# One change to the second block of a two-block network on one core: recurrence products as 64x64 pairs, filling products in runs of 12, attention heads in pairs, and the hand-over to the expert stage rearranged

## The chip, the core and the metric

The program runs on one core of a Trainium2 chip. A core has a matrix engine (PE, TensorE), three engines for elementwise work (DVE, ACT, POOL) and SP, which here only issues DMAs. Each engine works through its own list of instructions strictly in the order in which the compiled program holds them; semaphores make one wait for another. The metric is device time in microseconds (us) of one execution of the whole program, the median of the runs shown.

## The reference

Two transformer-like blocks run over 256 tokens of width 1024, in float32. The first (half an FFN, a mixer of long convolution and differential attention, half an FFN) is not touched. The second block, reduced to what matters:

```python
u = rms_norm(x) @ w_in                      # 1920 recurrence columns, q, k, v, 2048 gates
# recurrence, 8 heads of 64, forward and reverse; S is 64x64 per head:
s_kk = S @ kk_t
S = S * w_t - outer(s_kk, a_t * kk_t) + outer(v_t, k_t);  y_t = S @ r_t
y_rwkv = (group_norm(y) * ln_w + ln_b + bonus) * g
# banded attention, 8 query heads of 64, 2 key heads, band of 128, ALiBi, a sink logit
y_attn = softmax_with_sink(q @ k.T + alibi) @ v
merged = sigmoid(g1) * (y_rwkv @ w_proj_rwkv) + sigmoid(g2) * (y_attn @ w_proj_attn)
x = x + merged @ w_out
x = x + expert_choice_moe(rms_norm(x))      # 16 experts, 32 tokens each, 3 weights of 1024x1024
return rms_norm(x)
```

## The kernel before

All activations stand feature by token: a tile is 128 features by 256 tokens. Large products are made exact by splitting: `split` (L138) takes a float32 tile, ACT casts a high part (`whi`, L139), DVE subtracts it (`wlo`, L140), and `mm3` (L142) issues three products (L145 high by high, L146 high by low, L147 low by high). A weight tile of 128 columns and 1024 rows so makes 24 products of 128x128 by 256 columns. `weights` (L125) loads it by one DMA on SP's queue (L130); its raw buffer is free for the next load but one as soon as DVE has made the low part.

**The recurrence** runs in chunks of 64 tokens. For each pair of heads (4 pairs, two heads on partitions 0 to 63 and 64 to 127) and each direction there is a "lane" (`lane`, L1255): decays by a matmul (L1270) and exponentials, products of keys with keys and queries (L1297), transposes (L1308), a triangular inverse (`inverse`, L1363: by blocks of 8 on DVE, then three doubling levels of matmuls), a chain over the four chunks (L1325 to L1345), and the output products. `mm_heads` (L1358) does a product for the two heads as two 64x64 products, one on each half of rows and columns of the array. Where a full 128x128 product is used instead (L1297, L1308, L1387, L1449), the two heads' data stand as diagonal blocks in zero-padded tiles (`bb`, `kh`, filled by ACT at L1291), or all 128 rows are turned at once and the halves copied out one by one (L1310, L1406). `rwkv_out` (L1416) follows each pair's second lane.

**Order.** Four slots hold a lane each; `lanes` (L1197) goes round them, takes one step of each, and after each step spends a credit (`FILL_RATE`) on the "fill": the 22 weight tiles of `w2_fill` (queries, keys and values, gates), 22 x 24 = 528 products that do not depend on the recurrence. `FILL` says in how many pieces a tile's 24 products are handed out. After eight lanes the slots take four attention jobs (`banded`, L1472), each a pair of query heads j and 4+j, one after the other. A list scheduler then sets the final order within each engine; it may pull ready products in between, so pieces of the fill are broken up further.

**Hand-over.** When the lanes end, their SBUF goes to a ring of 27 raw buffers (`moe_raw`), and SP's queue runs on: four tiles `w_proj_rwkv` (into the two old raw buffers), four `w_proj_attn`, eight `w_out`, then the experts' 201 MB in loads of 512 KB. Before the first projection the outputs `ur` and `q` are split (L1054, L1055) into the tiles `h2h` and `h2l`, four small constants are loaded by ACT's queue (L1061, L1064), the router weights `wr` are scaled on DVE (L1065), and the gates go through a sigmoid on ACT in four parts (L1071).

## Time and profile before

| | us |
|---|---|
| median of 3 runs | 1842.15 (1841.99 to 1846.56) |
| the profiled execution | 1840.64 |
| its span, first to last instruction | 1838.9 |
| lane stage, from the 36th fill product to the last | 1086.5 to 1303.3 |
| first `w_proj_attn` load, last `w_proj_rwkv` load | 1303.14, 1309.53 |
| first expert load, last expert load landed | 1317.07, about 1822 |

The profiled execution is one run, 1.5 us below the median; the span leaves out 1.7 us around it. A time such as 1303.15 is us from the span's start. A group of matrix instructions in the timeline merges neighbours of one line and tile; its us reach to the modelled end of the last, so consecutive groups overlap, and what a group cost is read from its start to the next group's start. A float32 product (lines 1270 to 1505) shows as two PE instructions, a transpose and a split product as one. "PEclk" is the granted clock of TensorE, 1.00 for 2.4 GHz, 0.5 for 1.2 GHz.

### The profile page before, as it was taken

What the parts mean: (1) busy time and instruction counts of PE and PEld (TensorE: products, weight loads), DVE (VectorE), ACT (ScalarE), POOL (GpSimd) and SP (SyncE); (2) the same over time, 40 slices, a digit from 0 to 9 for tenths busy, and PEclk for the clock granted to TensorE, in tenths of its full rate; (3) what the DMA queues carried; (4) which work ended last, traced back from release to release, by engine and by line L of the source; (5) the groups of instructions that cost most, each with busy time, mean ns of one, the idle gap of its engine ahead of it and who ended that gap; (6) DMA issues with size and microseconds to landing.
All of it is one profiled execution on the core that took longest, in us unless ns stands there. A gap on an engine that the chain in (4) does not pass through costs nothing.

```text
span 1838.9 us, 33002 instructions
## 1 busy us (share of the span) xinstructions
PE 1704.7 (93%) x13367; PEld 1279.1 (70%) x13367; DVE 1032.4 (56%) x2506; ACT 733.8 (40%) x1576; POOL 19.0 (1%) x37
## 2 busy tenths in 40 slices
PE   8999999999999999999999999999999878787666
PEld 5788787778988889999998888887975222222112
DVE  4888766769977877776657686867751000000001
ACT  4432223647545577475445654555550000000001
POOL 0000000000000000000000000000010000000000
PEclk9999999999999999999999999999999676657887
DMA  8666663324422224545552321111799999999997
GB/s 335 237 212 215 231 243 120 110 92 133 155 95 90 70 89 164 184 183 209 185 176 73 125 98 59 47 44 42 281 400 392 409 408 409 408 409 408 409 408 295
DMA packets 98915, 397.77 MB, mean 216 GB/s; under 512 B 12251, under 2 KB 14924, under 8 KB 85196
## 3 DMA queue, kind: packets, MB, share of 16 engines
q1 hardware_dynamic: 91728, 386.97, 55.9%
q10 hardware_dynamic: 5020, 5.04, 0.9%
q0 software_dynamic: 2016, 3.67, 0.7%
q8 instruction: 105, 1.72, 0.4%
q14 instruction: 46, 0.38, 0.1%
HBM read 394.59 MB, written 1.05 MB: 215 GB/s over the span
## 4 chain that ended last, share of the span: by engine, by line
PE 68%; DMA 21%; DVE 6%; ACT 3%; issue 1%; ACTq 0%; SPq 0%; DVEq 0%
PE mm L145 14%; PE mm L147 13%; PE mm L146 13%; DMA raw<-exp_w_down 7%; DMA raw<-exp_w_gate 6%; DMA raw<-exp_w_up 4%; PE at L145 4%; PE a L1361 4%; PE at L146 4%; PE at L147 4%; PE mm L1530 3%; DMA araw<-w_adat 2%; PE a L1698 2%; DVE ajunk L309 2%; DVE wlo L140 1%
## 5 line engine op out<-in xcount | busy, mean ns | idle before, releaser
L139 ACT CAST whi<-raw 128x512 fp32r<-128x512 f32 x542 | 309.6, 619 | 260.2 <-PE mm L146 126.8
L140 DVE TENSOR_TENSOR wlo<-raw,whi 128x512 fp32r<-128x512 f32 x542 | 356.7, 687 | 89.2 <-ACT whi L139 85.8
L145 PE MATMUL mm<-hh,whi 128*128 128x256 f32 (+1 forms) x784 | 247.8, 317 | 0.4 <-DVE kl L140 0.4
L147 PE MATMUL mm<-hh,wlo 128*128 128x256 f32 (+1 forms) x784 | 247.1, 317 | 0.5 <-DVE wlo L140 0.2
L146 PE MATMUL mm<-hl,whi 128*128 128x256 f32 (+1 forms) x784 | 246.7, 315 | 0.0
L145 PEld LDWEIGHTS mm<-hh,whi 128*128 128x128 f32 x784 | 147.9, 189 | 14.0 <-issue 3.2
L146 PEld LDWEIGHTS mm<-hl,whi 128*128 128x128 f32 x784 | 147.9, 189 | 10.9 <-issue 1.2
L147 PEld LDWEIGHTS mm<-hh,wlo 128*128 128x128 f32 x784 | 147.3, 189 | 10.9 <-DVE wlo L140 1.3
L1665 DVE TENSOR_SCALAR scat<-iota,col 128x256 f32<-128x256 f32 x16 | 6.5, 413 | 260.2 <-PE a L1698 260.2
L1530 PE MATMUL mm<-raw,ehid 128*32 128x256 f32 x960 | 100.7, 515 | 40.6 <-DMA raw<-exp_w_down 40.2
L1702 ACT COPY ys<-mm 128x256 f32<-128x256 f32 (+1 forms) x20 | 7.2, 361 | 318.6 <-PE mm L1530 307.0
L309 DVE SCALAR_TENSOR_TENSOR ajunk<-araw,scr 128x512 bf16<-128x512 f32 x160 | 110.4, 690 | 25.5 <-DMA araw<-w_adat 23.4
L145 PE MATMUL at<-hh,whi 128*128 128x512 f32 (+1 forms) x352 | 119.8, 340 | 0.0
L147 PE MATMUL at<-hh,wlo 128*128 128x512 f32 (+1 forms) x352 | 119.5, 339 | 0.0
L146 PE MATMUL at<-hl,whi 128*128 128x512 f32 (+1 forms) x352 | 119.4, 339 | 0.0
L1530 PE MATMUL mm<-raw,xg 128*32 128x256 f32 x1024 | 101.3, 486 | 12.9 <-DMA raw<-exp_w_gate 12.5
L1530 PE MATMUL a<-raw,xg 128*32 128x256 f32 x1024 | 84.4, 462 | 23.7 <-DMA raw<-exp_w_up 23.7
L145 PE MATMUL mm<-whi,hidh 128*128 128x512 f32 x264 | 105.5, 400 | 0.4 <-DVE y L431 0.3
L147 PE MATMUL mm<-whi,hidl 128*128 128x512 f32 x264 | 105.0, 399 | 0.3 <-DVE hidl L140 0.3
L146 PE MATMUL mm<-wlo,hidh 128*128 128x512 f32 x264 | 105.0, 398 | 0.0
L145 PE MATMUL mm<-h2h,whi 128*128 128x256 f32 x328 | 102.2, 312 | 2.8 <-ACT h2h L988 1.7
L1530 PEld LDWEIGHTS mm<-raw,ehid 128*32 128x32 f32 x960 | 23.5, 123 | 114.5 <-DMA raw<-exp_w_down 96.9
(603 smaller groups left out, 3421.5 us busy)
## 6 DMA issues: line engine op xcount, KB each, us to landing
raw<-exp_w_gate SPq DMA_DIRECT2D x128, 512.0 KB, 10.2
raw<-exp_w_up SPq DMA_DIRECT2D x128, 512.0 KB, 10.2
raw<-exp_w_down SPq DMA_DIRECT2D x120, 512.0 KB, 10.2
raw<-w_ff_in SPq DMA_DIRECT2D x42, 1024.0 KB, 4.8
raw<-w_in SPq DMA_DIRECT2D x32, 1024.0 KB, 4.8
araw<-w_adat SPq DMA_DIRECT2D x56, 512.0 KB, 4.6
raw<-w_ff_out SPq DMA_DIRECT2D x20, 1024.0 KB, 4.8
raw<-w_fill SPq DMA_DIRECT2D x22, 512.0 KB, 3.5
```

The costliest lines, as they stand in the source:

```text
L139: self.high = self.nc.scalar.copy(out=hi, in_=src)
L140: self.low = (eng or self.nc.vector).tensor_tensor(out=lo, in0=src, in1=hi.bitcast(F32), op=ALU.subtract)
L145: nc.tensor.matmul(out=ps, lhsT=w[0], rhs=x[0], start=first, stop=False)
L146: nc.tensor.matmul(out=ps, lhsT=w[0], rhs=x[1], start=False, stop=False)
L147: nc.tensor.matmul(out=ps, lhsT=w[1], rhs=x[0], start=False, stop=last)
L309: nc.vector.scalar_tensor_tensor(out=junk, in0=raw[:, s], scalar=1.0, in1=self.scr[v][:, s], op0=ALU.mult, op1=ALU.mult, accum_out=part[:, ...
L1361: self.nc.tensor.matmul(out=ps[r], lhsT=w[r], rhs=x[r], start=start, stop=stop)
L1530: nc.tensor.matmul(out=ps[q], lhsT=x(k), rhs=raw[:, j, :], start=(k == 0), stop=(k == KT - 1))
L1665: nc.vector.tensor_scalar(out=sc, in0=self.iota[:, 0:T], scalar1=col[:, 0, e:e + 1], scalar2=col[:, 1, e:e + 1], op0=ALU.is_equal, op1=ALU ...
L1698: nc.tensor.matmul(out=acc(tt, j), lhsT=sc[q, tt * 128:tt * 128 + 128], rhs=ys[q], start=False, stop=False)
L1702: nc.scalar.copy(out=ys, in_=ps)
```

## The change

1. **64x64 pairs.** The zero-padded tiles `bb` and `kh` and their eight memsets go; key products use `mm_heads` on `t0` and `t1` directly. Transposes become products with the identity, head by head (`turn_heads`, new). The coefficient product (L1387) and the bonus sum (L1449) become pairs. One copy of 128 partitions stands where there were two of 64.
2. **Last doubling level.** Only half of each 64x64 inverse is still unknown there, so its two products take 32 columns. A tile `ip`, identity plus that half, replaces `P`; POOL writes the identity half, one copy per lane.
3. **Fill.** `FILL, FILL_RATE` go from 4, 0.31 to 2, 0.16: pieces of 12 products instead of 6, half as often. With `whole`, the 2nd to 4th quarter of a piece have high priority in the scheduler, so that it keeps the 12 together.
4. **Attention.** The two heads of a job run together, with products on the two row halves (queries by keys) and the two column halves (by values) side by side in the list, and one copy of the output.
5. **Hand-over.** `h2h`/`h2l` become 16 tiles of 128x256, the outputs are split one such tile at a time, the constants go to POOL's queue, each sigmoid is written where its gates are first used, and `wr` is scaled after the first projection.

```diff
-FILL, FILL_RATE = 4, 0.31
+FILL, FILL_RATE = 2, 0.16
...
-                    self.mm3(ps, (hi[:, k, s], lo[:, k, s]), (x[0][:, k, :], x[1][:, k, :]), k == 0, k == kt - 1)
+                    with self.tc.high_priority() if whole and k % (kt // steps) else ExitStack():
+                        self.mm3(ps, (hi[:, k, s], lo[:, k, s]), (x[0][:, k, :], x[1][:, k, :]), k == 0, k == kt - 1)
...
-            self.split(ur[:, 8:12, :], yr[0], yr[1])
-            self.split(q, ya[0], ya[1])
+            for y, x, i in ((yr, ur, 8), (ya, q, 0)):
+                for k in range(4):
+                    self.split(x[:, i + k, :], y[0][:, k, :], y[1][:, k, :])
...
-            nc.scalar.dma_start(out=t, in_=A[nm])
+            nc.gpsimd.dma_start(out=t, in_=A[nm])
...
-        for dst, src in ((bb, t0), (kh, t1)):
-            for r in HEADS:
-                nc.scalar.copy(out=dst[r, :, r], in_=c4(src)[r])
...
-                nc.tensor.matmul(out=ps[:, c], lhsT=src[:, c, :], rhs=kr[:, :, c * 64:c * 64 + 64], start=True, stop=True)
+                self.mm_heads(ps[:, c], src[:, c, :], kr[:, :, c * 64:c * 64 + 64])
...
-                nc.tensor.transpose(out=ps[:, c, :], in_=src[:, first + c, :], identity=self.ident)
-            for r in HEADS:
-                nc.scalar.copy(out=dst[r, cs], in_=ps[r, :, r])
+                self.turn_heads(ps[:, c, :], src[:, first + c, :])
+            nc.scalar.copy(out=dst[:, cs], in_=ps)
...
+    def turn_heads(self, ps, x):
+
+        for r in HEADS:
+            self.nc.tensor.matmul(out=ps[r], lhsT=x[r], rhs=self.ident[r, r], start=True, stop=True)
...
+        nc.vector.tensor_tensor(out=IP[:, :, src], in0=products(ab, N, src), in1=mask(8)[:, :, src], op=ALU.mult)
+        yield
+        nc.scalar.copy(out=NT[:, :, dst], in_=products(IP, NT, dst))
...
+        for qt in range(2):
+            for g, r in enumerate(HEADS):
+                nc.tensor.matmul(out=ps[g][:, qt, :], lhsT=q[r, j, qt * 128:qt * 128 + 128], rhs=kv[r, 0, :], start=True, stop=True)
```

PE, first lanes, before: 128x128 products and transposes with the padded tiles (`a` is PSUM, `krs` keys and queries, `vtm` the values).

```order
L1297 MATMUL a_10986<-krs_10897,bb_10886 128x128 x4
L1297 MATMUL a_10994<-krs_10897,kh_10888 128x128 x4
L1297 MATMUL a_11077<-krs_10916,bb_10905 128x128 x2
L1308 MATMUL a_11016<-ident,bb_10886 128x128 x3
L1297 MATMUL a_11077<-krs_10916,bb_10905 128x128 x2
L1297 MATMUL a_11099<-krs_10916,kh_10907 128x128
L1308 MATMUL a_11022<-ident,kh_10888 128x128 x3
L1361 MATMUL a_11039<-vtm,ak_10891 64x64 x2
L1297 MATMUL a_11099<-krs_10916,kh_10907 128x128 x3
L1361 MATMUL a_11039<-vtm,kt_10895 64x64 x2
```

The same place now (L1364 is `mm_heads`, L1369 `turn_heads`).

```order
L1364 MATMUL a_10992<-krs_10908,t0s_10910 64x128 x8
L1364 MATMUL a_11004<-krs_10908,t1s_10911 64x128 x8
L1364 MATMUL a_11093<-krs_10926,t0s_10928 64x128 x3
L1369 MATMUL a_11015<-ident,t0s_10910 64x64 x6
L1364 MATMUL a_11093<-krs_10926,t0s_10928 64x128 x4
L1369 MATMUL a_11023<-ident,t1s_10911 64x64 x6
L1364 MATMUL a_11042<-vtm,ak_10901 64x64 x2
L1364 MATMUL a_11093<-krs_10926,t0s_10928 64x128
L1364 MATMUL a_11113<-krs_10926,t1s_10929 64x128 x3
L1364 MATMUL a_11042<-vtm,kt_10905 64x64 x2
```

Every product of this stretch has become 64x64; over the lane stage the neighbours on PE differ in block shape (128x128, 64x64, 64x128, 128x64) 124 times instead of 237, and the 528 fill products stand in 49 runs instead of 101, most of them of 12.

DVE, end of the lanes, before: the low parts of the weights, then `wr`, then the split of `ur` and `q`, then the first projection's output (L1075).

```order
L1454 TENSOR_TENSOR ur<-t0s_10956,a_13781 128x256
L140 TENSOR_TENSOR wlo<-raw,whi 128x512 x4
L1065 TENSOR_TENSOR wr<-wr,pv 128x128
L140 TENSOR_TENSOR h2h<-ur,h2h 128x1024
L140 TENSOR_TENSOR h2l<-q_10151,h2l 128x1024
L140 TENSOR_TENSOR wlo<-raw,whi 128x512
L1075 TENSOR_TENSOR gates<-mm,gates 128x256
L140 TENSOR_TENSOR wlo<-raw,whi 128x512
```

Now (the four `wlo` are the halves of the first two projection tiles, L1470 is the last head pair's output).

```order
L140 TENSOR_TENSOR yl_14041<-q_10165,yl_14037 128x256
L140 TENSOR_TENSOR yl_14042<-q_10165,yl_14038 128x256
L1466 TENSOR_TENSOR t1s_10965<-ur,a_13872 128x256
L140 TENSOR_TENSOR yl_14043<-q_10165,yl_14039 128x256
L1467 TENSOR_TENSOR t0s_10964<-t0s_10964,t1s_10965 128x256
L140 TENSOR_TENSOR yl_14044<-q_10165,yl_14040 128x256
L1470 TENSOR_TENSOR ur<-t0s_10964,a_13877 128x256
L140 TENSOR_TENSOR wlo<-raw,whi 128x512 x4
L140 TENSOR_TENSOR yh_14036<-ur,yh_14032 128x256
L1081 TENSOR_TENSOR gates<-mm,gates 128x256 x2
L1092 TENSOR_TENSOR wr<-wr,pv 128x128
```

Most of the split now stands before the projection's weights, but the last recurrence output has moved behind the end of the fill; 58 fill products are left after the last lane's output products, where 114 were.

SP, the same place, before.

```order
L130 DMA raw<-w_fill 128x1024 x22
L130 DMA raw<-w_proj_rwkv 128x1024 x3
L130 DMA raw<-w_proj_attn 128x1024 x2
L130 DMA raw<-w_proj_rwkv 128x1024
L130 DMA raw<-w_proj_attn 128x1024 x2
L130 DMA raw<-w_out 128x1024 x8
```

Now.

```order
L130 DMA raw<-w_fill 128x1024 x22
L130 DMA raw<-w_proj_rwkv 128x1024 x4
L130 DMA raw<-w_proj_attn 128x1024 x4
L130 DMA raw<-w_out 128x1024 x8
L1545 DMA raw<-exp_w_gate 128x1024 x8
```

Two `w_proj_attn` loads have moved behind the last `w_proj_rwkv` load.

## Rows read from the trace of the kernel before

**Rows 1.** The page: shares of the chain that ended last.

```profile
PE 68%; DMA 21%; DVE 6%; ACT 3%; issue 1%; ACTq 0%; SPq 0%; DVEq 0%
```

**Rows 2.** Windows: us, then busy us (instructions) per engine; clock, DMA share, GB/s.

```profile
1086.50:1303.30 216.80, 212.28 (x2832) 175.90 (x2830) 154.43 (x545) 122.39 (x301) 0.00 (x0) 1.00 0.17 54
1303.30:1309.50 6.20, 4.29 (x22) 3.97 (x21) 4.19 (x6) 2.86 (x5) 0.00 (x0) 0.72 0.72 254
...
1365.00:1400.00 35.00, 34.00 (x353) 21.30 (x355) 12.41 (x39) 8.68 (x18) 5.06 (x8) 0.97 0.98 376
1400.00:1600.00 200.00, 164.80 (x1554) 54.55 (x1550) 9.23 (x22) 5.67 (x15) 0.00 (x0) 0.71 1.03 409
```

**Rows 3.** Timeline of SP's queue: start us, us, line, tile and source.

```profile
1303.14 0.86 SPq L130 DMA_DIRECT2D raw<-w_proj_attn  x2
1309.53 0.33 SPq L130 DMA_DIRECT2D raw<-w_proj_rwkv  x1
```

**Rows 4.** Timeline of PE: a run of six fill products inside the recurrence.

```profile
1133.15 0.52 PE L1361 MATMUL a<-Ws,ab 64*64 64x64 f32 x10
1133.59 0.39 PE L145 MATMUL mm<-h2h,whi 128*128 128x256 f32 x1
1133.82 0.28 PE L146 MATMUL mm<-h2l,whi 128*128 128x256 f32 x1
...
1134.29 0.28 PE L147 MATMUL mm<-h2h,wlo 128*128 128x256 f32 x1
1134.50 0.45 PE L1361 MATMUL a<-t0s,bt 64*64 64x64 f32 x8
```

**Rows 5.** Timeline of PE: pairs in a row, transposes between pairs, key products.

```profile
1106.14 0.68 PE L1361 MATMUL a<-Wvs,Ws 64*64 64x64 f32 x16
1106.65 0.63 PE L1361 MATMUL a<-Ws,Wvs 64*64 64x64 f32 x16
...
1119.93 1.05 PE L1297 MATMUL a<-krs,kh 128*128 128x128 f32 x8
1120.91 0.33 PE L1361 MATMUL a<-t0s,bt 64*64 64x64 f32 x4
...
1123.27 0.63 PE L1361 MATMUL a<-Ws,ab 64*64 64x64 f32 x14
1123.90 0.55 PE L1308 MATMUL a<-ident,kh 128*128 128x128 f32 x3
1124.38 0.33 PE L1361 MATMUL a<-ak,Ws 64*64 64x64 f32 x4
```

**Rows 6.** Lines of PE, 1086.5 to 1303.3: attention products; count, busy us, mean ns.

```profile
L1483 PE MATMUL a<-kv,q 64*128 64x256 f32 x32 | 9.8, 412 | 0.0
L1505 PE MATMUL a<-krs,v 128*64 128x256 f32 x32 | 8.6, 392 | 0.0
```

**Rows 7.** Waits of PE in that stretch, longest of eight kinds: us in all, times, longest.

```profile
PE a L1297 <- ACT bb L1291: 1.2, 1, 1.2
```

**Rows 8.** Lines of ACT in that stretch: copies that the change removes or halves.

```profile
L1291 ACT COPY bb<-t0s 64x256 f32<-64x256 f32 x16 | 6.5, 403 | 1.7 <-DVE t0s L1285 1.5
...
L1310 ACT COPY kt<-a 64x192 f32<-64x192 f32 x16 | 5.0, 313 | 3.0 <-PE a L1308 2.8
```

**Rows 9.** Timelines at the end of the fill: PE, then DVE.

```profile
1303.15 0.28 PE L145 MATMUL mm<-h2h,whi 128*128 128x256 f32 x1
...
1305.72 0.58 PE L146 MATMUL mm<-h2h,whi 128*128 128x256 f32 x1 [1.10 <-DVE h2h L140]
...
1304.24 0.29 DVE L1065 TENSOR_TENSOR wr<-wr,pv 128x128 f32<-128x128 f32 x1 [1.55 <-DMA wr<-w_router]
1304.45 1.22 DVE L140 TENSOR_TENSOR h2h<-ur,h2h 128x1024 fp32r<-128x1024 f32 x1
```

**Rows 10.** Lines of DVE in the lane stage: the two kinds of step at the hand-over.

```profile
L140 DVE TENSOR_TENSOR wlo<-raw,whi 128x512 fp32r<-128x512 f32 x43 | 29.1, 686 | 9.2 <-ACT whi L139 9.1
...
L1454 DVE TENSOR_TENSOR ur<-t0s,a 128x256 f32<-128x256 f32 x4 | 1.7, 420 | 1.0 <-PE a L1453 1.0
```

More of the change, by code (lines that the diff above doesn't have):

```diff
@@ L151, in gemm, with gemm_steps @@
             pass
-    def gemm_steps(self, src, x, n, consume, c0=0, c1=None, steps=1, ring=False):
+    def gemm_steps(self, src, x, n, consume, c0=0, c1=None, steps=1, ring=False, whole=False):
         i = 0
@@ L998, in block2 @@
         ph = self.pool("b2h", 1, es=es, side="left")
-        h = [ph.tile([128, KT, T], F32R, name=f"h2{q}") for q in "hl"]
+        h = [Columns([ph.tile([128, T], F32R, name=f"h2{q}{k}", tag=f"h2{q}{k}") for k in range(KT)]) for q in "hl"]
         gates = ph.tile([128, 16, T], F32, name="gates")
@@ L1069, in block2, with sigmoid @@
             mg = [pr.tile([128, KT, T], F32R, name=f"mg{q}") for q in "hl"]
-            for i in range(0, 16, 4):
+            def sigmoid(i):
                 nc.scalar.activation(out=gates[:, i:i + 4, :], in_=gates[:, i:i + 4, :], func=AF.Sigmoid)
@@ L1074, in p1_done @@
             def p1_done(m, ps):
+                if m % 4 == 0:
+                    sigmoid(m)
                 nc.vector.tensor_tensor(out=gates[:, m, :], in0=ps, in1=gates[:, m, :], op=ALU.mult)
             def p2_done(m, ps):
+                if m % 4 == 0:
+                    sigmoid(8 + m)
                 t = pr.tile([128, T], F32, name="mt", tag="mt", bufs=2)
@@ L1386, in inverse @@
         ps = self.pt(f"a{L['i']}", [128, 4, 8, 8])
-        nc.tensor.matmul(out=ps, lhsT=self.rc[:, 5, :], rhs=X, start=True, stop=True)
+        for r in HEADS:
+            nc.tensor.matmul(out=ps[r], lhsT=self.rc[r, 5, r], rhs=X[r], start=True, stop=True)
         nc.scalar.copy(out=coef, in_=ps)
@@ L1448, in rwkv_out @@
         ps = PS([128, T])
-        nc.tensor.matmul(out=ps, lhsT=rc[:, 4, :], rhs=b, start=True, stop=True)
+        for r in HEADS:
+            nc.tensor.matmul(out=ps[r], lhsT=rc[r, 4, r], rhs=b[r], start=True, stop=True)
         nc.vector.tensor_tensor(out=b, in0=ur[:, 8 + p, :], in1=ps, op=ALU.mult)
@@ L1497, in banded @@
+        nc.scalar.activation(out=e, in_=e, func=AF.Exp)
+        yield
+        nc.vector.tensor_tensor(out=z, in0=z, in1=e, op=ALU.add)
+        nc.vector.reciprocal(out=z, in_=z)
+        for g in range(2):
+            for qt in range(2):
+                nc.vector.tensor_scalar(out=S[g][:, qt, :], in0=S[g][:, qt, :], scalar1=z[:, g, qt:qt + 1], scalar2=None, op0=ALU.mult)
+            ps = PS(g, [128, 2, T])
             for qt in range(2):
                 for kt in range(2):
-                    nc.tensor.transpose(out=ps[:, kt, qt * 128:qt * 128 + 128], in_=s[:, qt, kt * 128:kt * 128 + 128], identity=self.ident)
@@ L1500, in banded @@
-            pT = L["kr"]
-            nc.scalar.copy(out=pT, in_=ps)
-            yield
-            ps = PS([128, T])
-            for kt in range(2):
-                nc.tensor.matmul(out=ps[r], lhsT=self.v2[:, kt, r], rhs=pT[:, kt, :], start=(kt == 0), stop=(kt == 1))
-            nc.scalar.copy(out=q[r, j, :], in_=ps[r])
-            yield
+                    nc.tensor.transpose(out=ps[:, kt, qt * 128:qt * 128 + 128], in_=S[g][:, qt, kt * 128:kt * 128 + 128],
+                                        identity=self.ident)
@@ L1510, in moe @@
+            nc.scalar.copy(out=pT[g], in_=ps)
+        yield
+        ps = PS(0, [128, T])
+        for kt in range(2):
+            for g, r in enumerate(HEADS):
+                nc.tensor.matmul(out=ps[r], lhsT=self.v2[:, kt, r], rhs=pT[g][:, kt, :], start=(kt == 0), stop=(kt == 1))
+        nc.scalar.copy(out=q[:, j, :], in_=ps)
+        yield
     def moe(self):
```

80 lines of the change are left out of this document (38 added, 42 removed).

## The prediction, made before the changed kernel was run

> **What bounds the kernel now.** I read the shares of the final chain first: PE two thirds, DMA a fifth [rows 1]. The windows by stage then say where each rules. In the lane stage PE is busy 212.3 of 216.8 us at full clock while the DMAs idle at 0.17 [rows 2]; from 1400 on it is the other way round, with DMA share 1.03 at 409 GB/s and the granted clock of TensorE at 0.71, because PE waits for expert weights [rows 2]. So there are two regimes: a lane stage as long as PE's list, then a stream of weights as long as its bytes. They meet in SP's queue. The last `w_proj_rwkv` load starts at 1309.53 and everything behind it, two attention tiles, eight `w_out` and the experts, could not be issued earlier [rows 3]. Between 1365 and 1400 the stream ran at 376 instead of 409 GB/s [rows 2], 35 x 33 / 409 = 2.8 us lost with the ring of buffers full. Otherwise it never pauses, so whatever the fill's end gains, the end of the program gains too, less what the hand-over loses.
>
> **Shape changes on PE.** This is the largest term. A run of six fill products stands between 64x64 work [rows 4]. Inside the run a product starts every 0.117 us (1133.82 to 1134.29, four steps). The first takes 0.23, and 0.21 pass from the start of the last to the next pair, so 0.11 and 0.09 too much. The ten instructions ahead of it take 0.44 us, while elsewhere sixteen take 0.51, 0.032 each [rows 5]: 0.32, so 0.12 too much. One visit, two changes of shape, costs 0.32 us, 0.16 per change. The same stands without a fill [rows 5]: fourteen instructions take 0.63 instead of 0.45 us before three transposes, 0.18 too much. The built lists hold 237 changes before and 124 after, from the 36th fill product (38th in the changed list) to the last. 113 x 0.16 = **-18.1 us**. Bounds: 0.10 (the 0.09 and 0.11 alone) and 0.18, so -11 to -20.
>
> **The products themselves.** The key products: eight instructions, four products, take 0.98 us (1119.93 to 1120.91); four pairs of twice 64 columns should take twice the 0.51 of four pairs of 64, 1.02. Sixteen groups x 0.04 = +0.6. The transposes: three take 0.48 with the change of shape in it, so 0.32 without. In all 80 transposes (L1308, L1404) x 0.107, a third of 0.32, = 8.6 become 160 products x 0.064 = 10.2: +1.6. The last doubling level keeps 128 products with half the columns. By columns that is 128 x 0.032 = -4.1, by instructions nothing; I take -2.0. Attention: 64 instructions in the two groups [rows 6]. No row starts two of these side by side, so I bound the price of one by 0.21 (half its mean, as the products of 64x64 in rows 5 show) and the saving by half of 64 x 0.21 = 13.4 and by nothing: -6.7 to 0; I take half, -3.4. Sum **-3.2 us**, range -10 to +2.
>
> The Trainium skill speaks against the attention and key pairs: the page TensorEngine Tiling (Array Packing), section Restrictions and Gotchas, has it that different row tiles cannot access the same PSUM bank at the same time, and each key pair writes the two partition halves of one bank. By that rule the halves would take turns. The trace disagrees for 64 columns: 0.064 us per product against 0.245 for a full one of 128 columns, half of which is 0.12 [rows 5]; the rule's case is a rival below. The same page, Performance Considerations, states an overhead of about 60 cycles per matmul, so that few columns cost as much as 60. By it the 32-column level would save nothing, an estimate of 0 where columns give -4.1; the sum would be 2 us higher. No row here shows 32 columns in this block shape.
>
> **Waits in the lane stage.** Eight kinds of wait hold PE, 4.2 us together, the longest 1.2 for ACT's copy into `bb` [rows 7], which goes: -1.0. Against that stands a tighter stage. DVE works 154.4 us there [rows 2] and loses next to nothing (the half level, 8 x 0.17). In 216.8 us that is 71%; in a stage of some 197 us it is 78%. ACT falls: 32 copies of 0.403 into `bb` and `kh` and 16 of the 32 of 0.313 go [rows 8], about 18 of 122 us. So DVE is late next, but not the bound on average. Runs of 12 also hold a lane's next product back by up to 12 x 0.117 + 0.32 = 1.7 us instead of 1.0, while three other lanes have work. I take +3 for new waits, bounds 0 and +9: **+2.0 us** net.
>
> **POOL.** Eight memsets before the lanes become eight copies within them, on an engine with no other work in the stage (0.00 in rows 2). Their readers come several DVE and PE steps later, so I price them at 0; if DVE were held for each, 8 x 0.5 = 4 us, which is inside the bound for waits.
>
> **The hand-over.** Before: last fill product starts 1303.15; DVE waits 1.55 us for the router weights that ACT's queue loaded late, only then makes the low part of `ur`, and PE resumes in earnest at 1305.72 [rows 9], at a granted clock of 0.72 over that window [rows 2]. The changed order takes away that wait, since POOL issues the constants before the lanes end and `wr` is scaled later. It adds another. The last lane finishes with 58 fill products left, not 114, and its output chain (a bonus product, two DVE steps, a gate product, a DVE step L1470) now lies behind the last fill product. Behind L1470 on DVE stand the low parts of both first projection tiles, and on ACT a sigmoid stands before the cast of the fourth `ur` tile. Following DVE after the fill's end: about 3.4 us to the end of L1470 (six splits, two of them by then done, and three steps, of 0.42 each with PE's two products between), then 4 x 0.69 for the low parts, then 0.42 for the last split [rows 10]. That is 6.2 us to the release of the fourth `w_proj_rwkv` load, where before it took 1309.53 - 1303.27 = 6.3 (1303.27 is the last fill product's start and its 0.12). But the third such load and two of `w_proj_attn` no longer go ahead of it: two more tiles behind it, 2 x 0.524 MB / 409 GB/s = 2.6 us. PE, too, gets its 24th projection product about 1.8 us later after the fill. Both ways **+2.5 us**; bounds 0 (the 2.8 us of full ring absorb it) and +6 (PE waits so long that its clock stays low for some further us).
>
> **Sum.** -18.1 - 3.2 + 2.0 + 2.5 = -16.8 us. The profiled execution was 1840.64 us (1838.9 span, 1.7 around it); it would be 1823.8. The median of the runs lies 1.5 above the profiled one, so I predict 1842.15 - 16.8 = **1825 us**. Ends of the terms: -20 - 10 - 1 + 0 = -31 and -11 + 2 + 8 + 6 = +5.
>
> **Rivals.**
> 1. *Larger gain.* Pairs overlap fully, the half level pays, the waits stay: -20 - 7 + 0 + 2 = -25, 1817. For it: PE has no waits worth naming now. Against: DVE at 80%. Chance 0.17.
> 2. *DVE becomes the bound in the two stretches where lanes start,* or the hand-over loses its 6 us: the shape term pays half, -9 - 3 + 5 + 3 = -4, 1838. For it: 154 us of DVE in strict order. Chance 0.17.
> 3. *Halves take turns* (the rule above). Each key product of one head then costs as much as a full one, 0.245, so a group 1.96 instead of 0.98: 16 x 0.98 = +15.7 in place of +0.6, and attention saves nothing: -17 + 15 + 3, about 1843, no change. Chance 0.04.
> 4. *Slower: the lanes starve.* The fill is handed out in twelves, a lane's next link waits for a whole run, the lanes end late, and when the fill is used up the last links run uncovered. A link of one pair and one DVE step shows as 0.33 us on PE and about 0.9 us in all; if the 0.72 us by which a run is longer fell on one chain at each of the 49 runs, that is +35 - 17, 1860. It decides from the point where more than half of the runs delay the only lane that is not waiting. Against it: the order keeps four slots alive until about the last 13 runs, and 58 fill products still follow the last lane. Chance 0.07.
>
> **How the numbers follow.** My case, -24 to -8, has 0.55. A difference under 0.3% (5.5 us) can't be told from none here. Faster: 0.55 + 0.17 + half of rival 2, 0.08, and some of it beyond that bound, so 0.84. Within: 0.09 from rivals 2 and 3. Slower: 0.07. The range for 8 in 10 leaves out the far end of rival 1 and all of 3 and 4: 1811 to 1839.
>
> **What would show it.** In the changed profile: key products and turns on 64x64 lines only; a fill run of 12 in about 1.6 us between pairs; the lane stage about 197 us and its last fill product near 1284; DVE near 78% and ACT near 53% busy in it; PE's waits under 13 us; the fourth `w_proj_rwkv` load about 6 us behind the last fill product with four `w_proj_attn` loads behind it; 409 GB/s from then on. Key products at 1.9 us per group would show rival 3, a PE idle by more than 15 us in the lane stage rival 2 or 4, and a stream that starts 17 us earlier but ends less than 12 us earlier would say that the end is not set by the stream.

## The result and the profile after

The changed kernel takes 1820.2 us (median of 4 runs, 1816.37 to 1822.08), the kernel before 1842.83 beside it: ratio 0.9883, interval 0.9864 to 0.9902. That is 22.6 us less, where 16.8 were forecast. The profiled execution of the changed kernel is the fastest of the four, 1816.37 us with a span of 1814.6, so the two traces differ by 24.3 us, and this is the difference that they must account for.

The windows of the changed kernel, columns as in [rows 2], with POOL's 3.73 us for its eight copies in the lane stage:

```profile
1086.50:1279.60 193.10, 190.51 (x3227) 166.58 (x3226) 149.48 (x544) 99.48 (x247) 3.73 (x8) 1.00 0.18 61
...
1365.00:1400.00 35.00, 33.89 (x484) 18.69 (x480) 3.36 (x8) 1.51 (x4) 0.00 (x0) 1.00 1.02 405
```

The lane stage is 193.1 us where it was 216.8, PE busy 190.5 of it, DVE 77% and ACT 52% (78% and 53% were forecast). The dip of the stream between 1365 and 1400, 376 GB/s in [rows 2], is gone.

SP's queue at the hand-over, to set beside [rows 3], and below it the last group of loads, first of the changed kernel, then of the kernel before:

```profile
1269.06 15.97 SPq L130 DMA_DIRECT2D raw<-w_proj_rwkv  x4
1285.12 1.81 SPq L130 DMA_DIRECT2D raw<-w_proj_attn  x4
...
1784.81 9.27 SPq L1545 DMA_DIRECT2D raw<-exp_down_last  x8
```

```profile
1807.86 9.70 SPq L1522 DMA_DIRECT2D raw<-exp_down_last  x8
```

A stretch that can be compared in all kernels runs from the start of the first lane's decay product (L1270 before, L1277 now) to the start of the last fill product. It begins before the first pairs and leaves out what ran earlier. Before and after:

```profile
1058.24:1303.15 244.91, 238.86 (x3064) 200.96 (x3061) 176.52 (x589) 136.05 (x330) 0.00 (x0) 1.00 0.20 64
```

```profile
1058.94:1279.47 220.53, 215.90 (x3449) 190.37 (x3446) 170.16 (x582) 112.16 (x272) 3.73 (x8) 1.00 0.21 71
```

So the traces split as follows. The stretch begins 0.7 us later; it is 24.4 shorter; from the last fill product to the start of the last load (a queue's group ends 0.33 behind that) it takes 514.3 where it took 514.1; and the tail behind is 0.8 shorter. 0.7 - 24.4 + 0.2 - 0.8 = -24.3. PE's idle time in the stretch went from 6.1 to 4.6 us.

In the timeline of PE a run of fill products between pairs now looks so, the pair behind it last:

```profile
1125.51 0.39 PE L145 MATMUL mm<-h2h,whi 128*128 128x256 f32 x1
1125.73 0.28 PE L146 MATMUL mm<-h2l,whi 128*128 128x256 f32 x1
...
1126.93 0.28 PE L147 MATMUL mm<-h2h,wlo 128*128 128x256 f32 x1
1127.14 0.68 PE L1364 MATMUL a<-Wvs,Ws 64*64 64x64 f32 x16
```

Twelve products take 1.63 us from 1125.51 to the next pair, first step 0.22 and last 0.21 as in [rows 4]. What each kind of product costs is read from its start to the next row's start:

```profile
1088.94 1.09 PE L1364 MATMUL a<-krs,t0s 64*64 64x128 f32 x16 [0.91 <-DVE krs L1295]
1089.86 1.04 PE L1364 MATMUL a<-krs,t1s 64*64 64x128 f32 x16
...
1106.29 0.68 PE L1364 MATMUL a<-Ws,ab 64*64 64x64 f32 x16
1106.81 0.52 PE L1369 MATMUL a<-ident,t1s 64*64 64x64 f32 x12
...
1109.83 0.66 PE L1364 MATMUL a<-Ws,ab 64*64 64x32 f32 x16
1110.32 0.31 PE L1364 MATMUL a<-vtm,ak 64*64 64x64 f32 x4
...
1121.16 0.56 PE L1369 MATMUL a<-ident,t0s 64*64 64x64 f32 x12
1121.56 0.28 PE L1364 MATMUL a<-Wvs,krs 64*64 64x64 f32 x4
```

A key group of eight 64x64 products takes 0.92 us (0.98 as four full ones, [rows 5]), three turned pairs 0.40 (three transposes 0.32, the forecast's 0.48 less a change of shape), sixteen instructions (eight products) of 64 columns 0.52, and sixteen of 32 columns 0.49. Attention, queries by keys: eight instructions in 1.07 us,

```profile
1219.60 1.13 PE L1499 MATMUL a<-kv,q 64*128 64x256 f32 x8
1220.67 0.38 PE L145 MATMUL mm<-h2h,whi 128*128 128x256 f32 x1
```

and DVE behind the end of the fill, whose last product starts at 1279.47:

```profile
1281.86 0.41 DVE L1470 TENSOR_TENSOR ur<-t0s,a 128x256 f32<-128x256 f32 x1
1282.19 2.49 DVE L140 TENSOR_TENSOR wlo<-raw,whi 128x512 fp32r<-128x512 f32 x4
1284.60 0.42 DVE L140 TENSOR_TENSOR yh<-ur,yh 128x256 fp32r<-128x256 f32 x1
```

The order is the one that was followed in the forecast: the last output (L1470), the four low parts, then the last split. The fourth `w_proj_rwkv` load goes at 1284.70, when the fourth low part is done (1284.68); it does not wait for the last split, which runs beside it. That is 5.2 us behind the last fill product's start (6.4 before by the same measure), or 5.1 behind its end, where 6.2 were forecast. PE's clock stays at 1.00 here, where it had fallen to 0.5 for 3.4 us.

### The profile page after: what moved, and what is told of

Same layout as the page of the kernel before. It is cut to its first block, busy times and chain, and to the rows that moved or that the text cites. A ratio compares the mean times of both kernels' runs of the same rounds, so it can differ in the third digit from the quotient of the medians.

```text
span 1814.6 us, 33724 instructions
## 1 busy us (share of the span) xinstructions
PE 1680.5 (93%) x13759; PEld 1271.1 (70%) x13759; DVE 1028.1 (57%) x2508; ACT 711.0 (39%) x1520; POOL 19.8 (1%) x41
## 4 chain that ended last, share of the span: by engine, by line
PE 74%; DMA 19%; DVE 3%; ACT 3%; issue 1%; ACTq 0%; SPq 0%; DVEq 0%
PE mm L145 15%; PE mm L147 14%; PE mm L146 14%; DMA raw<-exp_w_down 7%; DMA raw<-exp_w_gate 7%; PE at L145 4%; PE at L146 4%; PE at L147 4%; PE a L1364 4%; PE mm L1553 3%; DMA raw<-exp_w_up 3%; PE a L1721 2%; PE a L1553 1%; PE at L236 1%; ACT whi L139 1%
## 5 line engine op out<-in xcount | busy, mean ns | idle before, releaser
L147 PEld LDWEIGHTS mm<-hh,wlo 128*128 128x128 f32 x784 | 147.2, 188 | 11.1 <-DVE wlo L140 1.5
L1553 PE MATMUL mm<-raw,ehid 128*32 128x256 f32 x960 | 92.6, 477 | 47.1 <-DMA raw<-exp_w_down 46.7
L145 PE MATMUL mm<-h2h,whi 128*128 128x256 f32 x296 | 89.6, 303 | 1.8 <-ACT h2h L989 1.3
## 6 DMA issues: line engine op xcount, KB each, us to landing
raw<-exp_w_gate SPq DMA_DIRECT2D x128, 512.0 KB, 10.2
raw<-exp_w_up SPq DMA_DIRECT2D x128, 512.0 KB, 10.2
raw<-exp_w_down SPq DMA_DIRECT2D x120, 512.0 KB, 10.2
```

The source lines that it names most:

```text
L145: nc.tensor.matmul(out=ps, lhsT=w[0], rhs=x[0], start=first, stop=False)
L147: nc.tensor.matmul(out=ps, lhsT=w[1], rhs=x[0], start=False, stop=last)
L1553: nc.tensor.matmul(out=ps[q], lhsT=x(k), rhs=raw[:, j, :], start=(k == 0), stop=(k == KT - 1))
```

## The experiments

All in one table first. "Stretch" is first decay product to last fill product; "changes" are those of block shape on PE in it, from the built lists; "last load" is from the last fill product to the start of the last load; "half clock" is how long the granted clock stood at 0.5 between 1200 and 1400 us. Time is the median, and the ratio relates it to the kernel before as measured beside it (1842.8, 1840.4, 1841.3 and 1841.8 in the four sets of runs), so ratios compare better than times. Stretch, last load and half clock come from one profiled execution each. Kernels with the same lanes (changed, e4, e11) differ by up to 0.6 us in the stretch, so no more than that is no difference.

| kernel | stretch | changes | last load | half clock | time | ratio (interval) |
|---|---|---|---|---|---|---|
| before | 244.9 | 245 | 514.1 | 6.8 | 1842.8 | 1 |
| changed | 220.5 | 133 | 514.3 | 3.4 | 1820.2 | 0.9883 (0.9864 to 0.9902) |
| e1 fill only | 235.7 | 206 | 518.4 | 13.6 | 1836.9 | 0.9980 (0.9968 to 0.9993) |
| e2 old fill | 233.9 | 213 | 514.0 | 6.8 | 1831.5 | 0.9950 (0.9931 to 0.9968) |
| e3 old attention | 226.0 | 136 | 518.4 | 13.7 | 1824.0 | 0.9909 (0.9892 to 0.9925) |
| e4 old hand-over | 220.0 | 133 | 528.2 | 23.8 | 1830.3 | 0.9944 (0.9928 to 0.9961) |
| e5 full last level | 224.3 | 132 | 513.2 | 6.8 | 1822.3 | 0.9895 (0.9867 to 0.9924) |
| e6 listed head by head | 221.7 | 131 | 516.2 | 10.2 | 1818.9 | 0.9862 (0.9834 to 0.9891) |
| e7 runs of 24 | 219.9 | 109 | 513.3 | 3.4 | 1816.8 | 0.9856 (0.9830 to 0.9882) |
| e8 six buffers | 220.1 | 131 | 519.5 | 20.5 | 1821.6 | 0.9876 (0.9845 to 0.9907) |
| e9 runs of 24, busy router | 219.9 | 109 | 513.7 | 0 | 1817.0 | 0.9866 (0.9845 to 0.9887) |
| e10 six buffers, busy router | 220.1 | 131 | 514.8 | 3.4 | 1818.6 | 0.9871 (0.9853 to 0.9889) |
| e11 router weights early | 220.0 | 133 | 514.3 | 6.8 | 1821.0 | 0.9892 (0.9876 to 0.9909) |
| e12 hand-over only | 244.5 | 245 | 512.5 | 3.4 | 1842.4 | 1.0012 (0.9995 to 1.0029) |

### The fill alone, and all but the fill

The kernel before with the new fill:

```diff
-FILL, FILL_RATE = 4, 0.31
+FILL, FILL_RATE = 2, 0.16
...
+                    with self.tc.high_priority() if whole and k % (kt // steps) else ExitStack():
...
```

> The kernel before with the fill alone changed: pieces of 12 products, half as often, kept whole; nothing else. Its built list has 206 changes of block shape on PE from the first lane's decay product to the last fill product (245 before, 133 in the changed kernel) and 54 fill runs (101 and 49). Theory A, every change of shape costs 0.16 us and waits do not grow: the lane stage, 1086.5 to the last fill product, is 39 x 0.16 = 6.2 us shorter than the 216.8 of before, and the program about 6 us shorter, ratio 0.997. Theory B, what costs is a visit to the fill whatever stands on its other side, 0.32 us each: 47 x 0.32 = 15 us shorter, ratio 0.992. Theory C, longer runs hold the lanes up: PE's waits in the stage rise from 4.2 us by 3 or more, gain under 3 us.

The changed kernel with the old fill:

```diff
-FILL, FILL_RATE = 2, 0.16
+FILL, FILL_RATE = 4, 0.31
...
-        (..., FILL, whole=True)
+        (..., FILL)
```

> The changed kernel with the old fill: pieces of 6 at the old rate, not kept whole. Its list has 213 changes of shape (133 in the changed kernel) and 98 fill runs (49). Theory A, 0.16 us per change: lane stage 80 x 0.16 = 12.8 us longer than the changed kernel's 193.1, so about 206, and ratio to the kernel before about 0.995. Theory B, 0.32 us per visit to the fill: 49 x 0.32 = 15.7 longer, about 209. Theory D, the gain of the changed kernel is in the products themselves and not in their neighbours: lane stage under 197.

The stretch in the first and in the second:

```profile
1063.98:1299.64 235.66, 230.22 (x3064) 197.40 (x3060) 174.18 (x588) 136.56 (x330) 0.00 (x0) 1.00 0.20 66
```

```profile
1060.09:1293.94 233.85, 229.21 (x3456) 195.53 (x3452) 173.58 (x586) 111.78 (x271) 4.24 (x8) 1.00 0.21 68
```

In e2 80 more changes cost 13.3 us, 0.167 each: theory A (12.8) to half a microsecond. Theory B (15.7) is 2.4 off, theory D is refuted. In e1 39 fewer changes saved 9.2, where A gave 6.2 and B 15; neither fits alone. PE idles 5.4 us there (6.1 before), so theory C is refuted: long runs did not hold the lanes up. Worked out from the starts of all matrix instructions, its fill products take 8.4 us less than before with 47 fewer runs, 0.18 a run. The two halves of the change alone save 9.2 and 11.1, together 24.4: 4 us belong to neither. The lists say why: 39 and 32 changes go when one half is made, 112 when both are, since a run of 12 between pairs still meets full-size key products on the way unless these are pairs too. What e1 saves beyond 0.17 a change, some 2.7 us, stays open. Of its 9.2 us the program kept only 3.5 (ratio 0.9980): in its trace the last load comes 4.3 us later behind the fill, with the clock at 0.5 for 13.6 us.

The time of the fill products alone, from start to start, is steadier than the price of a change: e2's take 9.3 us more than the changed kernel's for 49 more runs, 0.19 a run, against 0.18 in e1. [rows 4] show 0.20 lost at the two ends of a run. What varies between e1 and e2 is the share of the lane products around the runs.

### Attention heads one after the other

The changed kernel with `banded` as it was:

```diff
-        for qt in range(2):
-            for g, r in enumerate(HEADS):
-                nc.tensor.matmul(out=ps[g][:, qt, :], lhsT=q[r, j, ...], rhs=kv[r, 0, :], start=True, stop=True)
+        for g in range(2):
+            r = slice(64 * g, 64 * g + 64)
+            ps = PS([128, 2, T])
+            for qt in range(2):
+                nc.tensor.matmul(out=ps[:, qt, :], lhsT=q[r, j, ...], rhs=kv[r, 0, :], start=True, stop=True)
...
```

> The changed kernel with the attention of before, one head after the other. 136 changes of shape (133 in the changed kernel). In the traces so far the attention products from start to next start took 17.1 us before (lines 1483 and 1505) and 10.4 in the changed kernel (lines 1499 and 1528). Theory A, two products on different halves of rows or of columns run side by side: lane stage about 7 us longer than 193.1. Theory E, halves take turns, and the smaller sum comes from where these products stand among others: under 2 us longer.

```profile
1220.74 1.13 PE L1499 MATMUL a<-kv,q 64*128 64x256 f32 x4
1221.80 0.39 PE L145 MATMUL mm<-h2h,whi 128*128 128x256 f32 x1
```

Four instructions take 1.06 us here, eight took 1.07 in the paired kernel: the two row halves run side by side entirely. The stretch is 5.5 us longer, of which the 3 changes of shape are 0.5. Theory A said 7, theory E under 2. A holds, somewhat smaller. The edit also puts the old softmax and its copies back; PE's idle time does not grow by it (4.2 us for 4.6).

### Attention products listed head by head

```diff
-        for qt in range(2):
-            for g, r in enumerate(HEADS):
+        for g, r in enumerate(HEADS):
+            for qt in range(2):
... (and the same for kt and the values)
```

> The changed kernel with the attention products of a job listed head by head (both query tiles of one head, then both of the other; the same for the values) where they alternate between the heads. Same products, same tiles. Lines 1499 and 1528 took 10.4 us from start to next start in the changed kernel, 17.1 with the heads in separate jobs. Theory A, two products run side by side only when neighbours in the list are on different halves of the array: of four products only the middle two can overlap, so about 14 us, +3.5 in the stretch from first decay to last fill product (220.5). Theory H, PE overlaps them whatever their order in the list, or the gain came from elsewhere: within 1 us of 220.5.

```profile
1219.42 1.14 PE L1499 MATMUL a<-kv,q 64*128 64x256 f32 x8
...
1233.06 0.43 PE L1528 MATMUL a<-krs,v 128*64 128x256 f32 x1
1233.07 0.43 PE L1528 MATMUL a<-p1s,v 128*64 128x256 f32 x1
...
1233.54 0.38 PE L1528 MATMUL a<-krs,v 128*64 128x256 f32 x1
...
1254.58 2.03 PE L1499 MATMUL a<-kv,q 64*128 64x256 f32 x8
```

In the list all four products of a group now stand head by head. The first group still takes 1.14 us to its modelled end (1.13 in the changed kernel); that at 1254.58 takes nearly twice as long, 2.03. The same group in a narrower view of PE, with its second head alone, and DVE:

```profile
1255.48 1.13 PE L1499 MATMUL a<-kv,q 64*128 64x256 f32 x4
```

```profile
1255.01 0.42 DVE L1470 TENSOR_TENSOR ur<-t0s,a 128x256 f32<-128x256 f32 x1
```

The second head starts 0.05 us after DVE has ended the last recurrence output (L1470, 1255.43), on which its first product waits: the step still reads the PSUM buffer that this head writes. So the halves are apart here because one had to wait, and not because of the list. Of the three groups of queries by keys that stand undivided, the other two (from 1219.42 and 1253.24) overlap. In the values' groups the tiles name the head: the second head's first product (`p1s`, 1233.07) starts 0.01 us behind the first head's first (`krs`, 1233.06) and 0.47 ahead of the first head's second (1233.54), which stands before it in the list. Between the halves of the array PE's starts thus did not keep to the order of its list, which the opening section calls strict.

Over all groups lines 1499 and 1528 take 11.4 us (10.4 when they alternate, 14 by theory A), and the stretch grows by 1.2. Theory A is refuted. H is right that the order in the list does not decide; its bound of 1 us is missed by 0.2. The whole program shows no difference.

### The last doubling level on all columns

```diff
-        for level in range(2):
+        for level in range(3):
...
-        nc.vector.tensor_tensor(out=IP[:, :, src], in0=products(ab, N, src), in1=mask(8)[:, :, src], op=ALU.mult)
-        yield
-        nc.scalar.copy(out=NT[:, :, dst], in_=products(IP, NT, dst))
```

> The changed kernel with the last doubling level on all 64 columns as before, without the tile of identity and half inverse. 132 changes of shape (133 in the changed kernel). In the changed kernel's trace a product of 32 columns of this level takes 0.027 us from start to start, one of 64 columns 0.030. Theory A (my term of 2.0 us between 0 and 4.1, time goes with columns): the stretch from the first decay product to the last fill product is 2 to 4 us longer than its 220.5. Theory G, such short products cost the same whatever their columns: within 0.8 us of 220.5, but for what the slightly other order of instructions does.

```profile
1058.85:1283.17 224.32, 218.16 (x3455) 190.92 (x3452) 174.00 (x587) 113.15 (x272) 2.54 (x4) 1.00 0.22 72
```

The stretch is 3.8 us longer, which looks like theory A, but the products do not show it. Start to start, the two kinds of product that the last level consists of take 25.96 us over all three levels with all columns, and 25.81 with half of the columns in the last level. Theory G holds for the products, with 0.15 us. Of the 3.8, 1.5 are PE's idle time (6.2 for 4.6), and the last head pair's output products lie inside the stretch here, which they leave in the changed kernel; the rest is spread over other lane products. The program's ratio can't be told from the changed kernel's.

### Runs of 24

```diff
-FILL, FILL_RATE = 2, 0.16
+FILL, FILL_RATE = 1, 0.08
```

> The changed kernel with the fill in runs of 24 handed out half as often again (FILL 1, rate 0.08). 109 changes of shape (133), 29 fill runs (49). Theory A, 0.16 us per change as two experiments with the fill have borne out: the stretch from first decay to last fill product 24 x 0.16 = 3.9 us shorter than 220.5, the program 3 to 4 us faster than the changed one (ratio to the kernel before 0.9865). Theory C, runs of 24 (2.9 us) hold the lanes up, a lane's next product waits for a whole run: PE's waits in the stretch rise by 4 us or more, and the gain is gone.

```profile
1061.85:1281.74 219.89, 214.07 (x3450) 190.91 (x3446) 172.76 (x584) 113.85 (x273) 3.73 (x8) 1.00 0.22 71
```

The stretch is 0.6 us shorter, not 3.9, which is within the scatter. Start to start the fill products take 3.9 us less for 20 fewer runs, 0.19 a run as in e1 and e2; but PE idles 1.2 us more, and lane products take the rest back. So theory C begins here, at runs of 24, with less than its 4 us. The median is 3.4 us below the changed kernel's and the intervals overlap.

### The hand-over on the new lanes

The changed kernel with the old hand-over:

```diff
-            for y, x, i in ((yr, ur, 8), (ya, q, 0)):
-                for k in range(4):
-                    self.split(x[:, i + k, :], y[0][:, k, :], y[1][:, k, :])
+            self.split(ur[:, 8:12, :], yr[0], yr[1])
+            self.split(q, ya[0], ya[1])
...
+            for i in range(0, 16, 4):
+                nc.scalar.activation(out=gates[:, i:i + 4, :], in_=gates[:, i:i + 4, :], func=AF.Sigmoid)
... (constants on ACT's queue, wr scaled ahead of the projections)
```

> The changed kernel with the old hand-over: whole tiles h2h and h2l, constants on ACT's queue, four sigmoids ahead of the projections, router weights scaled ahead of them. The lanes are as in the changed kernel (133 changes of shape). My forecast priced the new hand-over at 2.5 us against the old one with the old order of loads; in the traces the landing of the last expert load moved 2.7 us less than the end of the fill. Theory A, these 2.7 us come from the order (two more tiles behind the last w_proj_rwkv load, a last output behind the fill) and not from the edits of the hand-over: with the old code on the new lanes the stream starts later still, by the 1.5 us wait for the router weights and the long splits, the fourth w_proj_rwkv load stands 7 us or more behind the last fill product (5.1 in the changed kernel), and the program is 2 to 6 us longer than the changed one. Theory F, the new code costs the 2.7 us: this kernel is as fast as the changed one or up to 3 us faster.

PE's longest wait between 1280 and 1300, SP's longest between 1284 and 1300, DVE's timeline, two windows of the stream, and the issues on SP's queue and on ACT's in that kernel:

```profile
PE mm L145 <- DVE gates L1077: 6.9, 1, 6.9
```

```profile
SPq L130 <- DMA wr<-w_router: 7.9, 1, 7.9
```

```profile
1299.05 0.29 DVE L1067 TENSOR_TENSOR wr<-wr,pv 128x128 f32<-128x128 f32 x1 [9.66 <-DMA wr<-w_router]
```

```profile
1320.00:1340.00 20.00, 20.00 (x165) 19.21 (x164) 11.98 (x25) 11.53 (x29) 0.00 (x0) 1.00 0.94 362
1340.00:1360.00 20.00, 17.71 (x107) 12.50 (x106) 11.38 (x34) 10.57 (x32) 6.41 (x9) 0.83 0.75 272
```

```profile
1283.80 3.58 SPq L130 DMA_DIRECT2D raw<-w_proj_attn  x4
```

```profile
1285.49 0.45 ACTq L1066 DMA_DIRECT2D wr<-w_router  x1
```

The program is 10 us longer, more than theory A's 2 to 6, and theory F is refuted. The 2.7 us from which both theories start were misread. They compare the landings that end the final chain (1822.3 and 1801.3), and these are not the same load of the last group in both kernels. By the start of the last load it is 0.2 (514.1 and 514.3), and the last load before landed at 1827.4, not at about 1822.

The way there is another than expected: the fourth `w_proj_rwkv` load goes sooner (3.4 us behind the fill), so the stream is there first. ACT's queue issues the load of `wr` at 1285.5 behind a table load, a sigmoid, a cast and three other constants; it lands 13.5 us later (4.9 in the kernel before). DVE stands 9.7 us before it can scale `wr` and turn to the next gates, and PE waits 6.9 for these; its granted clock is 0.5 for 10.2 us from 1294.8. The stream stands as well: in the trace SP's fifth `w_out` load waits 7.9 us for the semaphore of the `wr` load and goes at 1299.04. Later the ring fills while PE is late, and the stream runs at 272 to 362 GB/s. The small load so held two lists, DVE's and SP's. How the 10 us divide between them was not tried; that the ring was full later speaks for PE's side.

Is it the queue of the constants, or the rest? The changed kernel with that part alone put back:

```diff
-            nc.gpsimd.dma_start(out=t, in_=A[nm])
+            nc.scalar.dma_start(out=t, in_=A[nm])
...
+        nc.vector.tensor_tensor(out=wr, ...)    (ahead of the first projection again)
```

> The changed kernel with one part of the old hand-over back: the four constants on ACT's queue and the router weights scaled on DVE ahead of the first projection. Splits by tile and the late sigmoids stay. Theory A, the 10 us that the whole old hand-over cost on the new lanes (1830.3 against 1820.2, with DVE waiting 9.7 us for the router weights, whose load now shared the DMAs with the stream) are this wait: 1828 to 1832. Theory N, the long splits of whole tiles and the four sigmoids made most of it: under 1824.

```profile
1286.12 0.46 ACTq L1067 DMA_DIRECT2D wr<-w_router  x1
```

```profile
1287.38 3.28 SPq L130 DMA_DIRECT2D raw<-w_proj_attn  x4
```

1821.0: no loss, theory A falls. The same load, issued on the same queue 1.3 us ahead of the attention tiles instead of 1.7 behind them, lands in 4.7 us, and the order puts the scaling behind three of the projection's gates, where it waits for nothing (it landed at 1290.84 and is scaled at 1291.00). SP does not wait for it either. So neither the queue nor the place in the source cost 10 us by themselves. What differs in e4 is that the small load stands behind the stream's first loads, at the head of DVE's list and in the way of SP's. With the rest of the new hand-over it does not, as e11 shows; whether the splits or the sigmoids see to that was not tried.

On the old lanes, the kernel before with this diff turned round:

```diff
-            self.split(ur[:, 8:12, :], yr[0], yr[1])
+                    self.split(x[:, i + k, :], y[0][:, k, :], y[1][:, k, :])
...
```

> The kernel before with the new hand-over alone: outputs split by tile, constants on POOL's queue, each sigmoid at its first use, router weights scaled behind the first projection; lanes, fill and attention as before. Theory A, on the old lanes the hand-over is worth the wait it removes, 1.55 us on DVE and 2 us of half clock on PE: 1 to 4 us faster than before, ratio about 0.9985. Theory O, it is worth what it was on the new lanes, 10 us: ratio about 0.9945. Theory F, it loses what my forecast priced it at, 2.5 us: ratio 1.0014.

No difference (1.0012, 0.9995 to 1.0029). O is refuted, and so is A for the time: its 0.9985 lies outside the interval, though 1.6 us show in the one trace (512.5 against 514.1 to the last load). F's 1.0014 lies inside, and the time can't tell it from no change; the trace speaks against a loss.

### Does the stream or PE set the end?

Six raw buffers, so that the stream need not wait for the fill's last weights:

```diff
-RAW, RAW2 = 27, 14
+RAW, RAW2 = 23, 18
-        self.weight_pool(2, 2)
+        self.weight_pool(6, 2)
... (ab, ak and hb, hk of a lane become halves of s1 and p1)
```

> The changed kernel with six raw weight buffers in the second block where there were two, paid for by letting four 64-column tiles of each lane slot share the attention's tiles, and by a ring of 23 and 18 raw buffers where it was 27 and 14. All four w_proj_rwkv loads can then be issued during the fill, and the stream no longer waits for the release behind the last fill product. Theory A, the end is set by the stream: it starts 5.2 us earlier and has two tiles (2 x 1.28 us) less, so the program is 6 to 8 us shorter than the changed one. Theory J, the stream and PE's way from the last fill product to the first expert are equally long, as the stream at 400 to 407 GB/s between 1340 and 1400 (409 when never full) suggests: the ring is full while PE is still at the router, and the gain is what PE waits for behind the fill, 2 to 3 us. Theory K: sharing tiles adds waits in the lanes, no gain.

```profile
1285.33 4.23 SPq L130 DMA_DIRECT2D raw<-w_out  x8
```

```profile
1320.00:1340.00 20.00, 19.56 (x158) 18.28 (x156) 7.84 (x16) 8.69 (x26) 0.52 (x1) 1.00 0.60 194
1340.00:1360.00 20.00, 18.16 (x59) 10.38 (x60) 10.81 (x38) 8.76 (x25) 5.92 (x8) 0.53 1.02 404
```

The first expert load goes 6.5 us behind the last fill product instead of 18.6, and nothing is gained: the stream falls to 194 GB/s between 1320 and 1340, its ring full, until PE comes. Theory A is refuted; J is right in kind, without its 2 to 3 us. K's waits in the lanes are not there (stretch 220.1). The ring is also four buffers smaller at first, 23 for 27, and so fills sooner; that was not separated.

`WARM` is the number of products without a purpose that PE works on at three places in the router. More of them, once with the six buffers (e10) and once with runs of 24 (e9):

```diff
-WARM = 4, 8, 4
+WARM = 6, 13, 7
```

> The kernel with six raw buffers (ratio 0.9876) with the same additional products in the router. There the stream began 12 us sooner behind the last fill product than in the changed kernel and then ran at 194 GB/s between 1320 and 1340 and at 307 between 1360 and 1380, and PE's clock stood at 0.5 for 20.5 us from 1341. Theory J, PE's way bounds the end: with the clock kept up the program is 4 to 8 us shorter than with six buffers alone, 1814 to 1818. Theory M, the ring of buffers is too small for a stream that starts early, whatever PE does: within 2 us of 1821.6.

> The changed kernel with fill runs of 24 and, in the router of the expert stage, more products without a purpose on PE (6, 13 and 7 where there were 4, 8 and 4), as many as fit into PE's three waits there (0.67, 1.33 and 0.65 us in the changed kernel). In every trace so far the granted clock falls to 0.5 for 3.4 to 20.5 us at about this place, after waits of PE. Theory J, PE's way from the last fill product to the first expert bounds the end together with the stream: without the fall of the clock, 1 to 3 us faster than runs of 24 alone (1816.8 against 1841.3 before, ratio 0.9856), so ratio about 0.984. Theory L, the stream alone bounds it once the fill has ended: no difference from 0.9856.

With six buffers:

```profile
1340.00:1360.00 20.00, 18.77 (x114) 11.62 (x118) 12.49 (x41) 10.16 (x28) 5.92 (x8) 0.91 1.02 403
```

Here the half clock shrinks from 20.5 to 3.4 us and the last load comes 4.7 us sooner behind the fill, as J says. The medians differ by 3.0 with overlapping intervals, less than J's 4 to 8 and more than M's 2, so the time decides neither. With runs of 24 the clock no longer falls at all, and nothing is gained, as L says (0.9866; J's 0.984 lies just outside the interval). Both fit one reading of the table: 512 to 515 us from the last fill product to the last load in every kernel whose clock was low for 6.8 us or less, wherever its stream began; 516 to 528 where it was low longer. By this reading up to some 7 us of half clock hide behind the stream, which sets the end, and beyond that PE does. It is argued from one execution of each kernel, and only e9 and e10 change the clock on purpose; that the end changes over at 7 us is not shown.

## Why the prediction was right, and where not

*Shape changes, -18.1.* Right in size: 0.167 per change in e2, and 112 fewer of them in the built lists over the stretch, 18.7 us. Two runs speak against one price per change: the fill alone gave more than its share (e1), and at runs of 24 the stretch kept next to nothing of 24 changes (e7). What holds in all three is 0.18 to 0.19 us a run within the fill.

*Products, -3.2.* The sum was nearly right, by luck: measured, its parts are -5.0, -0.15, -1.0 and +2.0, or -4.1, and none but the last is as forecast. Their range, too, should end at -8.6 and not at -10. Attention saved about 5.0 (5.5 in e3 less 0.5), not 3.4: of the two ends of its range, the one for full overlap was nearer. The half level saved 0.15 instead of 2.0. This agrees with the rule of the Trainium skill that was cited (TensorEngine Tiling (Array Packing), Performance Considerations), by which few columns cost as much as 60; the rows 0.49 and 0.52 us decide it. Key products saved 0.06 us a group where 0.04 were added, 1.6 over sixteen groups apart from the forecast. The turned pairs cost 0.08 a group of three, 2 us in all for 80, as forecast (1.6). The rival that halves take turns in a PSUM bank is refuted by the key products: 0.92 us a group, not 1.96. Attention, which the forecast counted among its cases, was none: the two heads' scores go to different PSUM tiles (`ps[g]`), and its products by the values stand on column halves, not row halves.

*Waits in the lane stage, +2.0.* Wrong, the step that failed: "Runs of 12 also hold a lane's next product back", for which +3 was taken. PE's idle time fell by 1.4 us in the changed kernel, and by 0.6 with the runs of 12 alone (e1). With four slots a run of 1.6 us raised no wait; the price appears at runs of 24, and there it is 1.2 us of idle time and dearer lane products (e7). The rival in which lanes starve does not show at runs of 12 at all. POOL's copies, priced at 0, held nobody up that the trace shows.

*Hand-over, +2.5.* Its parts were off in both directions. The load is released 1.2 us sooner than before where 0.1 was forecast: L1470 ended 2.7 us behind the fill and not 3.4, and the low parts took 2.4 and not 2.8. (The forecast's 6.2 is 3.4 + 4 x 0.69. The 0.42 of the last split, named in the same sentence, is not in it, rightly.) The experts' first load comes 4.7 us later behind the fill where 2.5 were forecast for the stream. But the end of the stream moved by 0.2 only. "The 2.8 us of full ring absorb it" was the lower bound, and it is what happened: 376 GB/s became 405, and SP's waits ahead of the first expert loads for the router's first transposes on PE, for DVE and for ACT fell from 8.1 us to 3.4 (between 1290 and 1420), by the same 4.7. What the forecast missed is that without the new code the new lanes would have lost 10 us (e4), since it priced the old wait for the router weights at the 1.55 us that it had in the old place.

*Sum.* The forecast held because its largest term did. In the traces the stretch gave -24.4 where -19.3 were forecast (shape, products, waits), the rest 0.1 where +2.5 were. Against the medians, -22.6, the miss is 5.8 us. 1820 is inside the range, and it lies between my case and rival 1. Of that rival's terms, full overlap is what the runs show and waits that do not grow nearly so (they fell); that the half level pays is not.

## What to carry to other kernels

Price each change of block shape on the matrix engine from the trace, count changes in the built order, and make neighbours alike on both sides: two edits that removed 39 and 32 changes alone removed 112 together. When a stage becomes shorter, look again at every small load that used to run ahead of a stream: behind the stream's first loads one took 13.5 us to land instead of 4.9, and it held the stream's own queue as well. And where a ring of buffers joins a stream to an engine, an earlier start of the stream is worth nothing for as long as the ring would be full anyway.

## What the runs showed of the hardware

- 80 more changes of block shape on PE, at a granted clock of 1.00, took 13.3 us, 0.167 each (e2); within the fill it was 0.18 to 0.19 us a run (e1, e2, e7).
- A load of 64 KB landed in 2.9 us in the lane stage (changed kernel), 4.7 just ahead of the attention tiles' loads (e11) and 13.5 when issued 1.7 us behind the first of them (e4).
- Sixteen instructions (eight products) of 64x64 by 32 columns took 0.49 us, by 64 columns 0.52.
- Products on the two row halves of the array overlapped fully (eight instructions in 1.07 us, four in 1.06), also when listed head by head (1.14 to the modelled end, 1.13 when they alternate); where the second head had to wait for DVE, the same eight took 2.03 (e6).
- Listed behind both of the first head's products, the second head's first product on the other column half still started 0.47 us ahead of the first head's second (e6).
- The granted clock fell to 0.5 in the router of the expert stage in every kernel but e9, for 3.4 to 20.5 us. With a few more products without a purpose there it stayed at 1.00 with runs of 24 (e9; 3.4 us at 0.5 in e7) and fell for 3.4 us instead of 20.5 with six buffers (e10, e8).
